# A two-layer encoder trunk on one core: the chunk loop pinned to a written order, with PSUM banks of their own for masked scores and copied keys

## The chip, the cores and the metric

The kernel runs on one core of a Trainium2 chip. The core has a matrix engine (TensorE, PE in the profile, its weight loads PEld), a vector engine (VectorE, DVE), a scalar engine (ScalarE, ACT), GpSimd (POOL) and SyncE (SP), which issues the DMAs. Each engine takes its instructions from a queue of its own, in order, and an instruction at the head of a queue that waits for another engine holds up everything behind it. The metric is the time of one execution on the device in microseconds (us). Three runs of the kernel before took 1314.47 to 1317.25 us, with a median of 1316.5.

## The reference

The input x has 1024 tokens of 1024 numbers. Layer 0 projects it once and feeds two branches. Branch A is a Conformer convolution (gate, depthwise convolution over 31 tokens, LayerNorm, swish). Branch B is RWKV-7 time mixing: 8 heads of 64, in both directions, with a state of 64 x 64 per head:

```python
def step(S, inp):
    r_t, w_t, k_t, v_t, kk_t, a_t = inp
    sa = jnp.einsum('dbhvk,dbhk->dbhv', S, -kk_t)
    S = (S * w_t[..., None, :] + sa[..., :, None] * (kk_t * a_t)[..., None, :]
         + v_t[..., :, None] * k_t[..., None, :])
    return S, jnp.einsum('dbhvk,dbhk->dbhv', S, r_t)
```

The results of the two directions are added, normalised per head (group norm), scaled, a bonus term is added, and each branch is multiplied with a gate. The two branches side by side go through one output projection, `l0_w_out`, of 1024 x 1024; its first 512 rows belong to the convolution branch and its last 512 rows to branch B. Then x becomes LayerNorm(alpha x + mixer(x)). Layer 1 is a bidirectional chunked gated linear attention with 4 heads, again with an output projection and a LayerNorm. Everything is in 32-bit floating point.

## The kernel before

**Stages.** `phase_a` projects x, does the convolution taps and prepares the operands of the recurrence, which it writes to DRAM (tensors `ak`, `br`, `vt`, that is `akd`, `brd` and `vtd` in the profile). `conv_norm` finishes branch A. The class `Delta` computes the recurrence in 16 chunks of 64 tokens. `mix0` normalises the result per head, projects it and finishes layer 0. `layer1` is the second layer.

**The recurrence in chunks.** For each chunk, direction d and pair of heads t (two heads e lie on the two halves of the partitions) a triangular system of 64 x 64 has to be inverted. `solve` and `system` build the systems in four batches of four chunks, `invert` inverts their 32 x 32 diagonal blocks by elimination (batch 2 on DVE, batch 3 on POOL, with transposes on DVE at L510, L530 and L531 and two copies on ACT at L535), and `join` combines the blocks of one chunk (L551, L556). Batches 2 and 3 are inverted within the chunk loop (`INVERT`).

`Delta.run` is the chunk loop. For chunk s it issues the loads of chunk s + 2 (`load`), the `chain` of chunk s, one or two joins, the `operands` of chunk s + 1, and `between(s)`. `operands` multiplies the chunk's keys with its queries: the tile `pk` (64 x 192 for each head: 64 columns that are the keys themselves, since q holds a unit matrix there, and 128 columns of scores) and the tile `pa`. DVE masks the scores of `pk` into `q` (L599), ACT copies the keys from the same tile (L600); of `pa`, DVE masks one half into `ga` (L602) and ACT copies the other into `at` (L603). `chain` then is a sequence of small matmuls: `pw` (L624), copied to `w` by ACT; `pu` (L630), copied to `u`; `pf`, the next state, which DVE multiplies with the decay into the top half of `rs` of the next chunk (L641); and `py`, the output, copied to `yst` and stored.

**Fill.** The output projection of the convolution branch is cut into 16 tiles (`ConvHalf`: 8 row tiles for each half of 512 columns; 12 matmuls `po` each, after a split of the input into a high and a low part, on ACT and POOL). Five (`EAGER`) run ahead of the loop, the others are put behind the chunks by `FILL`, two per chunk. The weights of a half (`owah`, `owal`) are staged in pieces of 256 KB through two buffers `ws` and split into a high part by ACT (L755) and a low part by DVE (L756) when the first tile of the half is written.

**After the loop.** `mix0` stages the other half of the output weights (`owbh`, `owbl`, eight pieces `ws`) and the first value block of layer 1 (`blk`, four pieces) through two buffers with the tag `owbs`. The function `by_head` in it takes its `hi` and `lo` tiles from the same two buffers. `rwkv` normalises one row tile: `yf + yb` on DVE (L898), two passes of `by_head` on PE, several steps on ACT and DVE, a product on POOL, and a split into `lh` and `ll`. The tiles are taken in the order 3, 4, 2, 5, 1, 6, 0, 7, since the middle ones need only the middle chunks of both directions. The SBUF pool of `mix0`'s weights (`m0w`) is allocated after the pools of the inversion (`bz`), of the convolution weights (`m0a`) and of the convolution tiles (`m0b`) have been released.

**What sets the order.** A scheduler orders the instructions of each engine from the order in which they are written, the dependencies and its own estimate of times; an instruction that it takes to be ready may be placed ahead of earlier written ones. `tc.keep_in_program_order(ins)` pins an instruction behind the instruction written before it on the same engine. In the kernel before this is used for the accumulating matmuls of `pf` and `py` and a few loads.

**PSUM.** Eight banks of 2 KB per partition: two for `pk`, systems and the first joins (`bmm`), one for `pa` (`bpa`), three for the chain (`bpc`), two for projection tiles and the later joins (`fps`).

Of the kernel before, what the change touches and what calls it, by code (L numbers as in the profile page):

```python
# [8 lines left out]
F32 = mybir.dt.float32  # L9
# [49 lines left out]
C_N = 928  # L59
# [13 lines left out]
def prog(tc, I, out, dbg=None):  # L73
# [42 lines left out]
    half = lambda h: Out(tc, E, I["wo0"][:, 0:NT, h * 512:h * 512 + 512], pw, "owa", 2)  # L116
# [4 lines left out]
    for s in range(4):  # L121
        delta.join(s)
# [7 lines left out]
    with tc.high_priority():  # L130
        for n in range(EAGER):
            conv.tile(0, n, nc.vector)
    rest = list(range(EAGER, 2 * KT))

    def fill(m):
        for n in rest[:m]:
            conv.tile(n // KT, n % KT)
        del rest[:m]

    def between(s):  # L140
        if s in INVERT:
            delta.invert(INVERT[s], bz)
        fill(FILL[s] if s < len(FILL) else 0)

    delta.run(between)
    fill(len(rest))
# [35 lines left out]
FILL = (0, 2, 2, 2, 2, 2, 2, 1)  # L182
# [269 lines left out]
class Delta:  # L452
# [8 lines left out]
    def __init__(self, tc, E):  # L461
# [3 lines left out]
        self.pm = pool(name="bmm", bufs=2, space=PSUM)  # L465
# [73 lines left out]
    def join(self, s):  # L539

        nc, pm = self.tc.nc, self.pm
# [4 lines left out]
        pool, tag = (pm, "mm") if s < 8 else (self.fp, "ps")  # L546
# [5 lines left out]
        for r0, r1 in rows:  # L552
            A.copy(xn[r1], ps[r1, 0])
        for u in range(U):
            for r0, r1 in rows:
                PE.matmul(ps[r0, 1, u], lhsT=xn[r1, u], rhs=xu[r1, u, 32:64], start=True, stop=True)  # L556
        for r0, r1 in rows:
            A.copy(xu[r0, :, 32:64], ps[r0, 1])

    def load(self, s):  # L560
# [7 lines left out]
        self.ops[s] = (ak, q)  # L568
# [8 lines left out]
    def operands(self, s):  # L577

        nc, cst = self.tc.nc, self.E["cst"]
        PE, V, A = nc.tensor, nc.vector, nc.scalar  # L580
        ak, q = self.ops[s]
        at = self.p2.tile([P, 2, NT, L], F32, name="at", tag="at")
        ga = self.p2.tile([P, 2, NT, L], F32, name="ga", tag="ga")
        self.ops[s] = (q, at, ga)
        for d in range(2):
            pa = self.pa.tile([P, NT, P], F32, name="pa", tag="pa")
            for h in range(2):
                pk = self.pm.tile([P, 2, 3 * L], F32, name="pk", tag="mm")
                ts = slice(2 * h, 2 * h + 2)
                for t in range(2):  # L590
                    for e, rw in enumerate(ROWS):
                        PE.matmul(pk[ROWS[1 - e], t], lhsT=ak[rw, d, 2 * h + t, 1], rhs=q[rw, d, 2 * h + t, e], start=True, stop=True)  # L592
                    for e, rw in enumerate(ROWS):
# [749 lines left out]
```

## Time and profile before

| what | value |
|---|---|
| median of three runs | 1316.5 us |
| the profiled execution | 1315.19 us |
| its span in the profile | 1313.3 us |
| granted clock of TensorE, mean | 0.955 |
| chunk loop | about 502 to 773 us |
| `mix0` after the loop | about 773 to 877 us |

A line of the profile names the line of the kernel, the engine, the operation, what is written and read (`out<-in`) with shapes, and how often. In a timeline the first two numbers are the start and the length in us; idle time of the engine ahead of an instruction, with what ended it, stands in brackets. In a list of waits the numbers are the total in us, the count and the longest. In a grouped line the numbers after the bar are the busy time in us, the mean of one in ns, and the idle time ahead with what ended it. A 32-bit matmul shows as two instructions.

### The profile page before, as it was taken

To read this page: it belongs to the slowest core of one execution; us is meant where nothing else is said; L and a number is where in the kernel's file an instruction comes from. 1 tells how busy PE (TensorE), PEld (TensorE's weight loads), DVE (VectorE), ACT (ScalarE), POOL (GpSimd) and SP (SyncE) were. 2 spreads that over 40 slices of the span, in tenths; PEclk is the share of its full clock that TensorE was granted. 3 is DMA by queue.
4 is the path that set the end of the run, shared out by engine and by line. 5 is a ranking of instruction groups with operands and counts; after the bars stand their busy time and mean duration, and the time that the engine had idled before them with its cause. 6 is when DMAs were issued, how large, how long until landed. Compare 5 with 4: busy or idle time off the path is not lost.

```text
span 1313.3 us, 26499 instructions
## 1 busy us (share of the span) xinstructions
PE 1200.0 (91%) x10824; PEld 986.1 (75%) x10824; DVE 861.1 (66%) x1435; ACT 583.2 (44%) x1165; POOL 431.5 (33%) x405
## 2 busy tenths in 40 slices
PE   7999998989998488599978998899999999999997
PEld 5887776767777357478857787777989999887785
DVE  5698999899835993252455779747685666442443
ACT  5545564645643424344345545346353524242221
POOL 1237857493826768201000013401020202010243
PEclk9999998989999688799989999899999999999999
DMA  6215343443798944247487656212111110131222
GB/s 222 65 49 142 123 135 114 121 135 114 216 265 225 228 134 130 57 116 194 127 240 176 171 149 198 95 61 81 33 33 33 41 41 16 33 97 49 112 97 80
DMA packets 203753, 155.92 MB, mean 119 GB/s; under 512 B 93132, under 2 KB 168268, under 8 KB 203376
## 3 DMA queue, kind: packets, MB, share of 16 engines
q1 hardware_dynamic: 203632, 154.24, 40.9%
q8 instruction: 85, 1.39, 0.5%
q14 instruction: 36, 0.29, 0.1%
HBM read 104.92 MB, written 49.28 MB: 117 GB/s over the span
## 4 chain that ended last, share of the span: by engine, by line
PE 52%; DVE 20%; DMA 10%; ACT 6%; issue 6%; POOL 4%; SPq 1%; POOLq 0%; DVEq 0%; ACTq 0%
PE ps L170 6%; PE ps L168 6%; PE ps L169 6%; PE po L168 4%; DVE acc L250 4%; PE po L169 4%; PE po L170 3%; DMA w<-w 2%; DMA ws<-wo 2%; PE psv L168 2%; PE psv L170 2%; PE psv L169 2%; PE po L1200 2%; PE pk L592 2%; PE pf L617 2%
## 5 line engine op out<-in xcount | busy, mean ns | idle before, releaser
L168 PE MATMUL ps<-xh,wh 128*128 128x512 f32 (+1 forms) x480 | 193.2, 405 | 10.4 <-ACT xh L755 6.3
L169 PE MATMUL ps<-xl,wh 128*128 128x512 f32 (+1 forms) x480 | 192.7, 402 | 0.4 <-DVE xl L756 0.4
L170 PE MATMUL ps<-xh,wl 128*128 128x512 f32 (+1 forms) x480 | 192.5, 402 | 0.1
L250 DVE SCALAR_TENSOR_TENSOR acc<-up,vec,acc 128x1024 f32<-128x1024 f32 x116 | 149.0, 1285 | 2.3
L168 PEld LDWEIGHTS ps<-xh,wh 128*128 128x128 f32 (+1 forms) x480 | 92.3, 192 | 33.8 <-ACT xh L755 6.8
L169 PEld LDWEIGHTS ps<-xl,wh 128*128 128x128 f32 (+1 forms) x480 | 92.7, 193 | 22.0 <-DVE xl L756 1.3
L170 PEld LDWEIGHTS ps<-xh,wl 128*128 128x128 f32 (+1 forms) x480 | 92.4, 192 | 21.6 <-DVE wl L756 0.6
L599 DVE TENSOR_TENSOR q<-pk,cst 64x256 f32<-64x256 f32 x128 | 53.5, 420 | 55.5 <-PE pk L592 37.6
L168 PE MATMUL ps<-x1h,w1h 128*128 128x512 f32 x224 | 88.9, 397 | 0.0
L170 PE MATMUL ps<-x1h,w1l 128*128 128x512 f32 x224 | 88.3, 394 | 0.0
L169 PE MATMUL ps<-x1l,w1h 128*128 128x512 f32 x224 | 88.3, 394 | 0.0
L793 DVE SCALAR_TENSOR_TENSOR xr<-xr,po 128x512 f32<-128x512 f32 x48 | 32.7, 682 | 71.6 <-PE po L170 70.7
L813 POOL TENSOR_TENSOR xr<-xr,lnr 128x1024 f32<-128x1024 f32 (+2 forms) x16 | 29.1, 1817 | 151.3 <-ACT xr L809 151.3
L1147 POOL TENSOR_TENSOR e<-zq,e 128x1024 f32<-128x1024 f32 x4 | 9.6, 2408 | 203.2 <-ACT e L1144 203.2
L756 POOL TENSOR_TENSOR wl<-w,wh 128x512 fp32r<-128x512 f32 (+1 forms) x30 | 44.3, 1475 | 90.4 <-ACT wh L755 81.6
L595 PE MATMUL pa<-q,ak 64*64 64x128 f32 x512 | 43.5, 294 | 25.4 <-ACT at L603 25.4
L592 PE MATMUL pk<-q,ak 64*64 64x192 f32 x512 | 58.3, 350 | 5.8 <-ACT q L600 5.8
L908 POOL TENSOR_TENSOR yf<-yf,gb 128x512 f32<-128x512 f32 x8 | 10.5, 1315 | 146.6 <-DMA ak<-akd 95.2
L168 PE MATMUL psv<-w1h,x1h 128*128 128x256 f32 x192 | 55.0, 286 | 1.1 <-DVE v1l L756 1.1
L170 PE MATMUL psv<-w1h,x1l 128*128 128x256 f32 x192 | 54.9, 286 | 0.0
L169 PE MATMUL psv<-w1l,x1h 128*128 128x256 f32 x192 | 54.8, 286 | 0.0
L755 ACT CAST wh<-w 128x512 fp32r<-128x512 f32 (+1 forms) x60 | 36.2, 605 | 37.7 <-PE ps L169 26.7
(350 smaller groups left out, 3254.3 us busy)
## 6 DMA issues: line engine op xcount, KB each, us to landing
w<-w SPq DMA_DIRECT2D x100, 256.0 KB, 3.1
brd<-br SPq DMA_DIRECT2D x16, 512.0 KB, 3.6
akd<-ak SPq DMA_DIRECT2D x16, 512.0 KB, 3.5
ak<-akd SPq DMA_DIRECT2D x16, 512.0 KB, 4.5
q<-brd SPq DMA_DIRECT2D x32, 256.0 KB, 4.9
vtd<-vt SPq DMA_DIRECT2D x32, 128.0 KB, 2.6
ws<-wo SPq DMA_DIRECT2D x16, 256.0 KB, 4.4
ab<-akd SPq DMA_DIRECT2D x16, 256.0 KB, 5.0
```

The costliest lines, as they stand in the source:

```text
L168: nc.tensor.matmul(ps, lhsT=lh, rhs=rh, start=first, stop=False)
L169: nc.tensor.matmul(ps, lhsT=lh, rhs=rl, start=False, stop=False)
L170: nc.tensor.matmul(ps, lhsT=ll, rhs=rh, start=False, stop=last)
L250: V.scalar_tensor_tensor(acc if i < KS - 1 else cv, up[:, i:i + T], w(i), acc, ALU.mult, ALU.add)
L592: PE.matmul(pk[ROWS[1 - e], t], lhsT=ak[rw, d, 2 * h + t, 1], rhs=q[rw, d, 2 * h + t, e], start=True, stop=True)
L595: PE.matmul(pa[rw, 2 * h + t], lhsT=ak[rw, d, 2 * h + t, 0], rhs=ur, start=True, stop=True)
L599: V.tensor_tensor(q[ro, d, ts, e, 64:], pk[ro, :, 64:], mask, ALU.mult)
L617: ins = PE.matmul(*args, **kw)
L755: nc.scalar.copy(hi, src)
L756: (eng or nc.vector).tensor_tensor(lo, src, hi.bitcast(F32), ALU.subtract)
L793: nc.vector.scalar_tensor_tensor(x[:, hs], x[:, hs], alpha, ps, ALU.mult, ALU.add)
L813: G.tensor_tensor(x[:, lo], x[:, lo], g[:, lo], ALU.mult)
```

## The change

**The written order.** Two small classes, `Pinned` and `Ordered`, wrap the matrix, vector and scalar engines so that each instruction issued through them is pinned. All of the chunk loop on these three engines goes through such wrappers: chain, scores, keys, joins, the projection tiles of the fill. SP and POOL instructions are not pinned, nor are those of `invert`. `chain`, `join` and `between` become generators, and `run` writes their parts interleaved.

**PSUM.** `operands` is replaced by `scores` (the 128 score columns `pk` and the tile `pa`, whose masks are now both on DVE, with a table that has ones in its first half, into one tile `ag`) and `keys` (the 64 key columns in a tile `pt`, copied by ACT). `pk`, `pa` and `pt` each take one of three banks of the pool `bmm`; the pool `bpa` goes. `pw` and `pu` become one tile for both directions, with one copy of 512 columns instead of two of 256.

**The fill.** `FILL` now has at most one tile per chunk, nine in all; two tiles are written after the loop, pinned, with the low part on DVE. A tile is begun in one chunk (loads, split), multiplied later in that chunk, and its sum is written in the next. The second half of the weights is staged two pieces at a time from chunk 3 to chunk 5 (`HALF`). The joins of chunks 4 to 7 take their bank from `fps` instead of `bmm`.

**After the loop.** The splits of the output weights and of the first value block in `mix0` are pinned too, behind what is written before them.

```diff
-        self.pm = pool(name="bmm", bufs=2, space=PSUM)
+        self.pm = pool(name="bmm", bufs=3, space=PSUM)
...
+    def scores(self, s, d):
+        cst, (PE, V, _) = self.E["cst"], self.engines
+        ak, q, ag = self.ops[s]
+        pk = self.pm.tile([P, NT, P], F32, name="pk", tag="mm")
+        pa = self.pm.tile([P, NT, P], F32, name="pa", tag="mm")
+        for t in range(NT):
+            for e, rw in enumerate(ROWS):
+                PE.matmul(pk[ROWS[1 - e], t], lhsT=ak[rw, d, t, 1], rhs=q[rw, d, t, e, 64:], start=True, stop=True)
+            for e, rw in enumerate(ROWS):
+                ur = q[rw, d, t, e].rearrange("p (w i) -> p w i", w=3)[:, 0::2]
+                PE.matmul(pa[rw, t], lhsT=ak[rw, d, t, 0], rhs=ur, start=True, stop=True)
+        for e in range(2):
+            ro = ROWS[1 - e]
+            V.tensor_tensor(q[ro, d, :, e, 64:], pk[ro], cst[ro, C_MS:C_MS + P].unsqueeze(1).broadcast_to([64, NT, P]), ALU.mult)
+        V.tensor_tensor(ag[:, d], pa, cst[:, C_AC:C_AC + P].unsqueeze(1).broadcast_to([P, NT, P]), ALU.mult)
+
+    def keys(self, s, d):
+        PE, _, A = self.engines
+        ak, q, _ = self.ops[s]
+        ps = self.pm.tile([P, NT, L], F32, name="pt", tag="mm")
+        for t in range(NT):
+            for e, rw in enumerate(ROWS):
+                PE.matmul(ps[ROWS[1 - e], t], lhsT=ak[rw, d, t, 1], rhs=q[rw, d, t, e, 0:64], start=True, stop=True)
+        for e in range(2):
+            A.copy(q[ROWS[1 - e], d, :, e, 0:64], ps[ROWS[1 - e]])
...
         for s in range(NCH):
+            more, nxt = s + 2 < NCH, s + 1 < NCH
+            other = between(s, fixed)
+            joins = [self.join(j, fixed) for j in (2 * s + 4, 2 * s + 5) if j < NCH]
+            go = lambda g: next(g, None)
+            chain = self.chain(s)
+            if more:
+                self.load(s + 2)
+            go(chain)                 # pw, copy to w
+            go(other)                 # inversion, sum of the last tile, split of the next
+            go(chain)                 # pf, first half
+            if nxt:
+                self.scores(s + 1, 0)
+            go(chain)                 # pu, copy to u
+            if nxt:
+                self.keys(s + 1, 0)
+            for j in joins[:1]:
+                go(j)
+            go(chain)                 # py, first half
+            go(chain)                 # pf, second half, decay
+            if nxt:
+                self.scores(s + 1, 1)
+            for j in joins[:1]:
+                go(j)
+            go(chain)                 # py, second half, copy to yst
+            if nxt:
+                self.keys(s + 1, 1)
+            for j in joins[1:]:
+                go(j)
+            go(other)                 # projection tile
+            for j in joins[1:]:
+                go(j)
+            for _ in other:
+                pass
...
+class Pinned:
+    def __init__(self, tc, engine):
+        self.tc, self.engine = tc, engine
+    def __getattr__(self, name):
+        return lambda *args, **kw: self.tc.keep_in_program_order(getattr(self.engine, name)(*args, **kw))
+
+class Ordered:
+    def __init__(self, tc):
+        self.tensor, self.vector, self.scalar = (Pinned(tc, e) for e in (tc.nc.tensor, tc.nc.vector, tc.nc.scalar))
+        self.gpsimd, self.sync = tc.nc.gpsimd, tc.nc.sync
...
-FILL = (0, 2, 2, 2, 2, 2, 2, 1)
+FILL = (1, 1, 1, 0, 0, 0, 1, 1, 1, 1, 1, 1, 0, 0, 0, 0)
+HALF = 3
...
     delta.run(between)
-    fill(len(rest))
+    fixed = Ordered(tc)
+    for n in rest:
+        conv.tile(n // KT, n % KT, fixed, fixed.vector)
...
-    proj = Out(tc, E, I["wo0"][:, NT:], wbp, "owb", 2)
+    fixed = Ordered(tc)
+    proj = Out(tc, E, I["wo0"][:, NT:], wbp, "owb", 2, nc=fixed)
...
-            split(nc, res[0][:, k:k + 2], res[1][:, k:k + 2], w)
+            split(nc if i else fixed, res[0][:, k:k + 2], res[1][:, k:k + 2], w)
```

(The words after `#` in the loop are added here.)

More of the change, by code (lines that the diff above doesn't have):

```diff
@@ L121, in prog @@
     for s in range(4):
-        delta.join(s)
+        for _ in delta.join(s):
+            pass
     for j in range(FIRST + 1, 2 * NT):
@@ new lines, in chain @@
+        for d, t, e in units:
+            PE.matmul(ps[ROWS[1 - e], d, t], lhsT=q[:, d, t, e, 64:128], rhs=rs[:, d, t, e], start=True, stop=True)
+        A.copy(f(w), f(ps))
+        yield
+        pf = s + 1 < NCH and tile("pf")
+        if pf:
+            for d, t, e in units:
+                PE.matmul(pf[ROWS[e], d, t], lhsT=q[:, d, t, e, 0:64], rhs=rs[:, d, t, e], start=d + t == 0, stop=False)
+        yield
+        ps = tile("pu")
+        for d, t, e in units:
+            ro = ROWS[1 - e]
+            PE.matmul(ps[ROWS[e], d, t], lhsT=xa[ro, d, t], rhs=w[ro, d, t], start=True, stop=True)
@@ L649, in chain @@
-        A.copy(yst.rearrange("p d t i -> p (d t) i"), ps)
-        nc.sync.dma_start(self.E["y"][s], yst)
+            PE.matmul(py[ROWS[e], d, t], lhsT=u[ROWS[e], d, t], rhs=ag[ROWS[e], d, t, 64:], start=False, stop=d + t == NT)
+        A.copy(f(yst), f(py))
+        self.tc.nc.sync.dma_start(self.E["y"][s], yst)
+        yield
     def run(self, between):
         tc, nc = self.tc, self.tc.nc
+        fixed = Ordered(tc)
+        self.engines = fixed.tensor, fixed.vector, fixed.scalar
         self.p2 = tc.alloc_tile_pool(name="b2", bufs=2, reuse_waits="tile", side="right")
-        self.pa = tc.alloc_tile_pool(name="bpa", bufs=1, space=PSUM, reuse_waits="tile")
@@ L759, with __init__ @@
 class Out:
-    def __init__(self, tc, E, w, pw, tag, stages=2, room=None):
-        nc = tc.nc
+    def __init__(self, tc, E, w, pw, tag, stages=2, room=None, later=None, nc=None):
+        nc = nc or tc.nc
         _, self.n, self.cols = w.shape
@@ L774, in __init__, with stage, fetch, cut @@
             for i, h in enumerate(hs):
-                ws = room.tile([P, 512], F32, name="gup") if room else pw.tile([P, 512], F32, name="ws", tag=tag + "s", bufs=stages)
-                nc.sync.dma_start(ws, w[:, k, h])
-                split(nc, *self.w[k][i], ws)
+                steps = self.stage(nc, w[:, k, h], self.w[k][i], pw, tag + "s", stages, room)
+                if later is None:
+                    steps[0]()
+                    steps[1](nc)
+                else:
+                    later.append(steps)
+    def stage(self, nc, src, dst, pw, tag, stages, room):
+        tile = []
+        def fetch():
+            if not tile:
+                tile.append(room.tile([P, 512], F32, name="gup") if room else pw.tile([P, 512], F32, name="ws", tag=tag, bufs=stages))
+                nc.sync.dma_start(tile[0], src)
+        def cut(nc):
+            fetch()
+            split(nc, *dst, tile[0])
+        return fetch, cut
     def norm(self, rows, pw):
@@ L1300, in layout @@
     cst[:, C_DM:C_DM + 32] = p % 32 < i[:, 0:32]
+    cst[:, C_AC:C_AC + P] = np.where(i < 64, 1, p % 64 <= i % 64)
     r["cst"] = cst
```

174 lines of the change are left out of this document (79 added, 95 removed).

## The prediction

> **What bounds the kernel now.** I read the page first, then the stages, then the waits inside the chunk loop. The page says that TensorE is busy nearly everywhere:
>
> ```profile
> span 1313.3 us, 26499 instructions
> PE 1200.0 (91%) x10824; PEld 986.1 (75%) x10824; DVE 861.1 (66%) x1435; ACT 583.2 (44%) x1165; POOL 431.5 (33%) x405
> ```
>
> That average covers stages with different limits, so here is the table by stage (the columns after the stretch are its length, then busy time and instructions of PE, weight load, DVE, ACT and POOL, then granted clock, DMA share and GB/s). The loop's first scores start at 502 and its last instructions end at 773; the second half of layer 0 runs from there to 877.
>
> ```profile
> 502.00:538.60 36.60, 21.28 (x469) 16.93 (x463) 10.76 (x19) 10.38 (x29) 29.26 (x56) 0.73 0.25 71
> 538.60:648.30 109.70, 108.83 (x2224) 87.31 (x2226) 44.46 (x95) 48.82 (x144) 9.47 (x8) 0.98 0.47 130
> 648.30:714.50 66.20, 51.49 (x1072) 43.28 (x1064) 35.35 (x78) 28.57 (x78) 0.00 (x0) 0.95 0.79 209
> 714.50:773.00 58.50, 56.79 (x1173) 44.86 (x1171) 40.52 (x94) 35.87 (x98) 4.18 (x4) 0.97 0.61 154
> 773.00:843.00 70.00, 60.87 (x320) 50.84 (x319) 61.92 (x123) 32.18 (x65) 27.72 (x17) 0.98 0.53 169
> 843.00:877.00 34.00, 30.96 (x193) 27.37 (x194) 16.09 (x36) 11.45 (x28) 3.52 (x4) 0.90 0.14 52
> ```
>
> The loop is bound by PE except in two places: the first row (15.3 us idle) and the third (14.7 us idle). DVE has more than half of its time free in the loop; from 773 to 843 it is the fullest engine, 61.9 of 70. The waits of the loop name the two holes:
>
> ```profile
> ACT q L600 <- DVE q L599: 39.8, 73, 2.3
> ...
> PE pa L595 <- ACT at L603: 16.4, 2, 15.3
> ...
> ACT owbh L755 <- DMA ws<-wo: 15.3, 6, 6.0
> ...
> PE pw L624 <- DVE q L599: 5.6, 6, 1.8
> ```
>
> The first hole is one wait: two copies of the last inversion stand in ACT's queue ahead of the copy that PE needs, and wait for POOL's elimination to end.
>
> ```profile
> 536.04 2.11 ACT L535 COPY xa<-xa 32x1024 f32<-32x1024 f32 x2 [14.37 <-DVE xa L531]
> ```
>
> The second is the staging of the output weights (casts to owbh) that hold ACT up for a DMA in the middle of the loop. The 39.8 us in which ACT waits for DVE on one score tile, because both read the same bank, cost PE little: it waited for those masks 5.6 us in all.
>
> **The change, part by part.** *The matmuls of a chunk.* The row below is a chunk late in the loop: it starts at 726.50 and the next at 738.45, 11.95 us, of which three matmuls of the next stage (the two of L891 and L890 in this fence and one more) take near 0.36 each, 1.1, so 10.85.
>
> ```profile
> 726.50 0.80 PE L624 MATMUL pw<-rs,q 128*64 128x64 f32 x18
> 727.23 0.50 PE L891 MATMUL pv<-lo,one 128*128 128x512 f32 x1
> 727.56 0.40 PE L890 MATMUL pc<-hi,cen 128*128 128x512 f32 x1
> ...
> 728.26 0.87 PE L592 MATMUL pk<-q,ak 64*64 64x192 f32 x8
> 729.06 0.33 PE L624 MATMUL pw<-rs,q 128*64 128x64 f32 x2
> ...
> 732.80 0.69 PE L617 MATMUL pf<-rs,q 128*64 128x64 f32 x16
> 733.41 0.68 PE L617 MATMUL pf<-u,at 64*64 64x64 f32 x16
> ...
> 735.48 1.15 PE L617 MATMUL py<-q,rs 128*64 128x64 f32 x32
> 736.56 0.97 PE L617 MATMUL py<-ga,u 64*64 64x64 f32 x26
> ...
> 738.45 0.80 PE L624 MATMUL pw<-rs,q 128*64 128x64 f32 x18
> ```
>
> Starts give the rates: 32 matmuls of 64 columns in 736.56 - 735.48 = 1.08 us, 34 ns each; eight of 192 columns alone in 0.80, 100 ns each. After the change a chunk has 224 matmul instructions of 64 columns (pw, pu, pf, py, and 32 for the keys, which leave the wide pk): 7.6 us. The 64 of 128 columns (scores) lie between 34 ns (2.2 us) and two thirds of the 100 ns (4.3 us); written in one order, four quadrants in turn, I take 40 ns, 2.5 us, near the low end because the rate of the narrow ones is mostly issue. Sixteen pf matmuls between two changes of tile shape take 0.61 us where 16 at 34 ns would take 0.54: a change costs 0.07 us. The old order has some 20 changes a chunk, the written one four to eight: 0.4 us. Together 10.5 us, 0.35 less than that chunk; the keys' own matmuls take back most of what fewer changes give. The Trainium skill, TensorEngine Tiling (Array Packing), Key Properties, says that switching the tiling mode drains TensorE; the trace agrees, with those 0.07 us. By that rule the sum stands as it is; if the 0.07 us were no drain and stayed with the matmuls, a chunk would be about 1 us longer and the sum 15 us later.
>
> *Joins and convolution tiles.* A half join and a projection tile, by the starts of what follows:
>
> ```profile
> 564.60 0.69 PE L556 MATMUL pj<-xa,xn 32*32 32x32 f32 x32
> 565.23 0.68 PE L630 MATMUL pu<-w,xa 64*64 64x64 f32 x16
> ...
> 571.88 0.50 PE L168 MATMUL po<-owah,lh 128*128 128x512 f32 x1
> ...
> 574.84 0.45 PE L624 MATMUL pw<-rs,q 128*64 128x64 f32 x8
> ```
>
> 0.63 us a half, 1.26 a join; 2.96 us a tile. The new loop holds 12 joins (15 us), 9 tiles (26.6), 15 full chunks (157.5), a last one without scores and state (5.5) and the first scores (3.5): 208 us. To this I add idle time: 10 of the 15.3 us at the inversion (ACT's pinned work after step 2 is placed behind the inversion's copies, and those are themselves free to be placed early, as before; behind them in ACT's queue stand the copies of w, u and the keys, and PE waits for those; ends 0 and 15), and 6 us of short waits, the 1.7 in 58.5 us of the fourth row scaled up. So 224 us where 271 were: **the loop ends 47 us earlier, near 726** (ends 37 and 62).
>
> *DVE and ACT in a chunk.*
>
> ```profile
> L599 DVE TENSOR_TENSOR q<-pk,cst 64x256 f32<-64x256 f32 x128 | 53.5, 420 | 55.5 <-PE pk L592 37.6 <-ACT q L600 16.3
> L793 DVE SCALAR_TENSOR_TENSOR xr<-xr,po 128x512 f32<-128x512 f32 x9 | 6.2, 685 | 17.9 <-PE po L170 17.9
> ```
>
> Six masks of 512 elements at 0.69 replace eight q masks and two ga masks at 0.42: 4.1 us for 4.2. With four decays (1.7) DVE needs 5.8 us in 10.5 and stays hidden; the copies of w and u, merged to 512 elements, take some 0.6 us and lie under pf's first half and the scores (over 3 us of PE). Their banks no longer change hands between DVE and ACT; what this frees is in the short waits. Three banks instead of two for the early systems, the larger table and the earlier residual load I cost at nothing: DVE's eliminations set the pace there. If that cover is gone it is a microsecond or two, either way.
>
> *What leaves the loop.* This part decides. The splits of the output weights (8) and of the first value block (4) are now pinned on ACT and DVE behind the last two projection tiles, and those behind the last chunk. In the old run the first weight load went out as soon as the last projection tile had read its weights, which lie in the same memory:
>
> ```profile
> 652.03 0.39 PE L170 MATMUL po<-owah,ll 128*128 128x512 f32 x1
> ...
> 653.09 1.02 SPq L776 DMA_DIRECT2D ws<-wo  x2
> ```
>
> No load had started earlier though SP had room, so I take it that loads must wait for that tile again, now the last thing after the loop. First the tail: ACT split, DVE split, 2.96 of PE, sum, the second split pinned behind that sum, 2.96 of PE: 10 us. That is an estimate from 2 x 2.96 and five short ACT and DVE steps. Then 12 staged pieces of 256 KB through two buffers. The nearest row is the same pattern on a quiet machine, eight pieces for layer 1:
>
> ```profile
> 877.13 15.92 SPq L1036 DMA_DIRECT2D w<-w  x8
> ...
> 896.58 0.69 DVE L756 TENSOR_TENSOR w1l<-w,w1h 128x512 fp32r<-128x512 f32 x1 [1.22 <-ACT w1h L755]
> ```
>
> 877.13 to 897.27 is 20 us, 2.5 a piece: 30 us. The head normalisation (rwkv in the second half) uses the same two buffers for its hi and lo parts, so it starts only then; its six loads a tile go with it, but land while the weights are staged. One tile's chain, two by-head passes through ACT, DVE and PE, took 17 us in the busy loop (734.52 to 751.5); with the engines to itself I take three quarters of that, 13 us.
>
> ```profile
> 731.09 1.12 DVE L907 SCALAR_TENSOR_TENSOR yf<-yf,vec,bv 128x128 f32<-128x128 f32 x4
> ...
> 734.52 0.69 DVE L898 TENSOR_TENSOR yf<-yf,yb 128x512 f32<-128x512 f32 x1 [1.08 <-DMA yb<-yd]
> ...
> 750.85 0.68 DVE L756 TENSOR_TENSOR ll<-yf,lh 128x512 fp32r<-128x512 f32 x1
> ...
> 773.42 0.40 PE L168 MATMUL po<-owbh,lh 128*128 128x512 f32 x1
> ```
>
> Before, the output projection began at 773.42, directly at the loop's end, with four tiles normalised. Now it begins 10 + 30 + 13 = **53 us after the loop** (ends 32, if the hi and lo parts get their buffers first, and 62). After that DVE has 3.4 more tiles to normalise than before, at 4.5 us (five instructions near 0.69 and the four of 1.12 together): 15 us on the engine that filled 61.9 of 70 us there; with 8 us free, **12 us** later (7 to 15).
>
> The long idle stretch has a price of its own: after the old 4.90 us wait the first eight pk matmuls took 1.54 us where 0.87 is usual.
>
> ```profile
> 675.58 1.54 PE L592 MATMUL pk<-q,ak 64*64 64x192 f32 x8 [4.90 <-ACT q L600]
> ```
>
> The Trainium skill, TensorE: Matmul & The Clock Gate, Part 1, has the array at half its clock after some 3.4 us idle until it has been busy as long; the trace agrees (0.73 granted in the first row of the loop). By that rule the sum would be 2 us higher; I leave it inside the range.
>
> **The sum.** -47 + 53 + 12 = +18 us on the profiled execution's 1315.2 (span 1313.3 and 1.9 around it; the median of the runs is 1.3 higher): 1333.
>
> **The rivals.** *Handover overlapped, faster.* If the hi and lo parts take buffers as they come free and only the eight output weights are needed, projection starts 32 us after the loop and DVE adds 7: -8, 1307; without the inversion's stall -18, 1297. For it: DVE and ACT are half empty while pieces land. Against: the loads are older in the program and fill both buffers at once. It decides from a handover below about 40 us with the loop as forecast. *No stall at the inversion.* Chunks 0 and 1 with joins and tiles are 33 us of PE, just the time that POOL needs up to 536; ordered well they cover it: 8 to 10 us less, 1324. *The written order itself waits.* From the end of pf to pw's second half PE has 3.4 us of work (scores 1.25, py's second half 1.08, keys 0.54, pw's first half 0.54); DVE needs four decays and two masks in that time, 3.06 us and the hand-offs. It just fits, and PE may no longer take other work meanwhile: 1 us a chunk is 15 us, 1348. That the order gains nothing on PE (10.85 a chunk, not 10.5) belongs here, +5 us.
>
> **How the numbers follow.** Forecast 0.42 (1333, its own range 1325 to 1342), overlapped handover 0.27, no stall 0.18, waiting order 0.13. Within 0.2% (2.6 us, about what a measurement of this kernel can tell from no change) lies a little of the second and third, 0.08; faster 0.30; slower 0.62. Leaving out a tenth at each end: 1296 to 1352.
>
> **What would show it.** Right: chunk starts (pw) 10 to 11 us apart without tiles and joins; no owbh casts between chunks; the last yst copy near 726; then PE nearly empty for some 45 us while ws lands, with the first po on owbh near 779; layer 1's start 15 to 20 us later than 877. Wrong: owbh casts or yf adds ahead of the last chunk, the loop ending before 705, or a gap behind it under 40 us.

## The result, and the profile after

The changed kernel takes 1331.5 us (median of four runs, 1326.4 to 1333.5) against 1315.5 beside it (1312.4 to 1317.3): 1.0119 times as long, 95% interval 1.0083 to 1.0154. The profiled execution took 1331.9, 16.7 more than the one before, where 18 were forecast. Its page:

```profile
span 1330.1 us, 27402 instructions
PE 1166.5 (88%) x11336; PEld 974.5 (73%) x11336; DVE 860.7 (65%) x1373; ACT 563.2 (42%) x1037; POOL 431.9 (32%) x403
PE   7999998889989575799997068799999999999997
```

TensorE works 33.5 us less than before and the run is longer: the "06" in the 40 slices is a stretch from 732 us on in which it stands still (slices of 33.3 us). The stages (columns as in the prediction): the rest of the loop from its second half chunk of scores, the handover, and the output projection of the second half; the last row is the projection stage of the kernel before, between the same two projection matmuls.

```profile
495.10:718.60 223.50, 190.90 (x5372) 174.23 (x5372) 102.34 (x172) 78.07 (x176) 43.64 (x72) 0.92 0.51 131
718.60:774.70 56.10, 12.53 (x32) 6.57 (x32) 18.67 (x32) 16.07 (x27) 1.62 (x1) 0.61 0.57 175
774.70:873.20 98.50, 82.31 (x384) 67.86 (x385) 81.09 (x160) 45.42 (x90) 34.01 (x21) 0.86 0.47 143
```

```profile
773.40:853.40 80.00, 70.77 (x372) 59.75 (x371) 67.61 (x134) 33.83 (x70) 29.08 (x19) 0.96 0.49 158
```

So the 16.7 us are: loop ended 54.8 earlier (773.4 to 718.6), a handover of 56.1 where there was none, 18.5 more in the projection stage, and 3 won back behind it. The waits of the changed kernel, from the loop to the first projection, show the two places where TensorE stands, and the loads behind the second:

```profile
PE pu L738 <- ACT w L738: 21.0, 2, 20.3
...
PE pc L993 <- ACT hi L818: 34.7, 1, 34.7
ACT owbh L738 <- DMA ws<-wo: 30.1, 7, 10.1
```

*The loop's hole* is the old one, and longer. ScalarE's queue, then what TensorE waited for:

```profile
536.20 2.11 ACT L552 COPY xa<-xa 32x1024 f32<-32x1024 f32 x2 [22.13 <-DVE xa L548]
538.34 0.74 ACT L738 COPY xa<-pj 32x256 f32<-32x256 f32 x2
539.10 0.58 ACT L738 COPY w<-pw 128x512 f32<-128x512 f32 x1
```

```profile
539.73 1.97 PE L738 MATMUL pu<-w,xa 64*64 64x64 f32 x32 [20.25 <-ACT w L738]
```

The copies of the last inversion stand ahead of the second chunk's copy of w. They end at 538.3; before the change they ended at 538.15. GpSimd sets that time (VectorE, whose transposes the copies read, waits 19.9 us for its elimination), so whatever TensorE saves ahead of it only lengthens the hole.

*A chunk* late in the loop, without tiles or joins, now takes 702.84 - 693.29 = 9.55 us, of which TensorE is busy 9.14:

```profile
693.29 0.80 PE L738 MATMUL pw<-rs,q 128*64 128x64 f32 x18
...
695.99 0.33 PE L738 MATMUL pk<-q,ak 64*64 64x128 f32 x2
...
696.91 1.10 PE L738 MATMUL pu<-w,xa 64*64 64x64 f32 x32
697.84 0.63 PE L738 MATMUL pt<-q,ak 64*64 64x64 f32 x16
...
702.84 0.80 PE L738 MATMUL pw<-rs,q 128*64 128x64 f32 x18
```

```profile
693.30:702.80 9.50, 9.14 (x291) 8.72 (x288) 5.67 (x11) 3.18 (x8) 0.00 (x0) 1.00 0.51 136
```

*The handover*, in order of time: last output of the loop, first load of a weight, its cast, then SyncE's queue ahead of the seventh load, that load's cast, the first head normalisation, and the first projection:

```profile
718.01 0.58 ACT L738 COPY yst<-py 128x512 f32<-128x512 f32 x1 [1.56 <-PE py L738]
...
726.47 0.81 SPq L852 DMA_DIRECT2D ws<-wo  x2
...
729.76 1.22 ACT L738 CAST owbh<-ws 128x512 fp32r<-128x512 f32 x2 [10.13 <-DMA ws<-wo]
...
739.47 1.64 SPq L985 DMA_DIRECT2D gb<-gbd  x1
...
743.39 0.45 SPq L852 DMA_DIRECT2D ws<-wo  x1
...
747.90 0.62 ACT L738 CAST owbh<-ws 128x512 fp32r<-128x512 f32 x1 [5.24 <-DMA ws<-wo]
...
760.49 0.62 ACT L818 CAST hi<-yf 128x512 fp32r<-128x512 f32 x1 [0.81 <-DVE blk L738]
761.16 0.79 PE L993 MATMUL pc<-hi,cen 128*128 128x512 f32 x1 [34.72 <-ACT hi L818]
...
774.72 0.80 PE L184 MATMUL po<-owbh,lh 128*128 128x512 f32 x1 [0.98 <-ACT lh L818]
```

Three parts one after the other: two convolution tiles to 726.5, staging to 760.5, one normalisation to 774.7. The wait of 34.7 us ends when a buffer of the staged weights comes free for hi.

### The profile page after: what moved, and what is told of

Read it like the earlier page. It is cut to its first block, busy times and chain, and to the rows that moved or that the text cites. A ratio compares the mean times of both kernels' runs of the same rounds, so it can differ in the third digit from the quotient of the medians.

```text
span 1330.1 us, 27402 instructions
## 1 busy us (share of the span) xinstructions
PE 1166.5 (88%) x11336; PEld 974.5 (73%) x11336; DVE 860.7 (65%) x1373; ACT 563.2 (42%) x1037; POOL 431.9 (32%) x403
## 5 line engine op out<-in xcount | busy, mean ns | idle before, releaser
L738 DVE TENSOR_TENSOR q<-pk,cst 64x512 f32<-64x512 f32 x64 | 44.0, 687 | 33.3 <-PE pa L738 26.6
L884 DVE SCALAR_TENSOR_TENSOR xr<-xr,po 128x512 f32<-128x512 f32 x37 | 25.3, 684 | 54.2 <-PE po L186 54.2
L185 PE MATMUL psv<-w1l,x1h 128*128 128x256 f32 x192 | 54.8, 286 | 0.0
L818 ACT CAST wh<-w 128x512 fp32r<-128x512 f32 (+1 forms) x60 | 36.2, 606 | 42.0 <-PE ps L185 25.3
L1011 POOL TENSOR_TENSOR yf<-yf,gb 128x512 f32<-128x512 f32 x8 | 12.3, 1536 | 124.7 <-DVE yf L1010 102.8
L819 POOL TENSOR_TENSOR ll<-ya,lh 128x512 fp32r<-128x512 f32 x9 | 11.4, 1270 | 125.8 <-ACT lh L738 125.8
L186 PE MATMUL po<-owch,ll 128*128 128x512 f32 x128 | 50.8, 398 | 0.0
```

What stands on the lines that cost most here:

```text
L185: nc.tensor.matmul(ps, lhsT=lh, rhs=rl, start=False, stop=False)
L186: nc.tensor.matmul(ps, lhsT=ll, rhs=rh, start=False, stop=last)
L738: return lambda *args, **kw: self.tc.keep_in_program_order(getattr(self.engine, name)(*args, **kw))
L818: nc.scalar.copy(hi, src)
L819: (eng or nc.vector).tensor_tensor(lo, src, hi.bitcast(F32), ALU.subtract)
L884: (nc or self.tc.nc).vector.scalar_tensor_tensor(x[:, hs], x[:, hs], alpha, ps, ALU.mult, ALU.add)
```

## The experiments

Twelve kernels, each timed against the kernel before on its own chip (its medians there: 1314.2 to 1316.3). Marks of the profiled execution, in us: start of the first pw, end of the loop's last copy (yst), start of the first and of the last projection matmul on owbh; then span, median, and the ratio to the kernel before with its interval.

| run | pw | yst | first po | last po | span | median | ratio |
|---|---|---|---|---|---|---|---|
| before | 505.2 | 773.4 | 773.4 | 853.4 | 1313.3 | 1315.5 | 1 |
| after | 498.1 | 718.6 | 774.7 | 873.2 | 1330.1 | 1331.5 | 1.0119 [1.0083, 1.0154] |
| e1 late copies | 494.8 | 708.1 | 763.8 | 859.9 | 1318.2 | 1321.3 | 1.0058 [1.0031, 1.0086] |
| e2 tiles early | 499.9 | 735.3 | 771.5 | 864.2 | 1321.2 | 1324.9 | 1.0068 [1.0045, 1.0092] |
| e3 written staging | 499.4 | 737.4 | 751.8 | 849.7 | 1306.3 | 1309.2 | 0.9946 [0.9922, 0.9970] |
| e4 no pins | 492.1 | 711.2 | 761.0 | 858.4 | 1315.2 | 1317.2 | 1.0009 [0.9986, 1.0031] |
| e5 own buffers | 496.7 | 719.0 | 751.0 | 847.5 | 1303.7 | 1310.4 | 0.9964 [0.9934, 0.9995] |
| e6 grouped | 500.4 | 745.8 | 800.9 | 897.7 | 1354.3 | 1354.9 | 1.0302 [1.0263, 1.0342] |
| e7 two early banks | 495.6 | 712.8 | 767.8 | 865.5 | 1322.9 | 1329.7 | 1.0115 [1.0066, 1.0164] |
| e8 combined | 495.7 | 715.5 | 723.4 | 815.2 | 1273.0 | 1274.7 | 0.9680 [0.9643, 0.9718] |
| e9 shared banks | 504.5 | 736.8 | 792.5 | 888.8 | 1344.5 | 1344.7 | 1.0211 [1.0172, 1.0250] |
| e10 shared, no pins | 494.5 | 732.0 | 778.3 | 876.9 | 1331.1 | 1329.5 | 1.0105 [1.0067, 1.0143] |
| e11 inversion alone | 498.9 | 699.4 | 754.3 | 851.9 | 1309.7 | 1311.6 | 0.9961 [0.9935, 0.9988] |
| e12 no pins, tiles early | 490.1 | 732.1 | 738.8 | 838.0 | 1294.8 | 1297.5 | 0.9869 [0.9831, 0.9907] |

**The hole at the inversion.** e1 pins the end of the inversion one step later:

```diff
+        if s == 2:
+            late.append(delta.invert(3, bz, fixed))
+            next(late[0])
+        if s == 3:
+            next(late[0])
...
+        yield
+        if fixed:
+            nc, V = fixed, fixed.vector
         V.memset(z.rearrange("p i j -> p (i j)")[:, ::33], 1.0)
```

> The end of the last inversion (one memset, two transposes, two copies on ScalarE) is pinned one step later, in step 3, where its result is still early; the elimination itself stays where it is. Theory: in the changed kernel these copies stand in ScalarE's queue ahead of the copy of w in the second chunk, and TensorE waits 20.25 us for that copy. The wait goes. What is late next: the low halves of the next two convolution tiles, which GpSimd computes behind the elimination (to 534), so the first tile's third matmul waits about 6 us instead. Net 14 us: loop 210 us instead of 223.5, 1318 us in all, with the handover after the loop unchanged at 56 us. Rival A, nothing is late next: 20 us, 1312. Rival B, TensorE waits for GpSimd's elimination by another way (the joins need it at once): no change, 1331.

The loop ended 10.5 us earlier, 10 us in the median. TensorE's wait for w is gone, and the next thing is late, as expected, by 8.3 us where 6 were expected:

```profile
532.41 0.80 PE L749 MATMUL po<-owah,ll 128*128 128x512 f32 x1 [8.28 <-POOL ll L830]
```

e11 makes the edit of e1 and takes that away too:

```diff
-        ahead = [conv.begin(n // KT, n % KT, fixed) for n in rest[:FILL[s]]]
+        ahead = [conv.begin(n // KT, n % KT, fixed, fixed.vector if s < 3 else None) for n in rest[:FILL[s]]]
```

> The changed kernel with the late copies of the last inversion, and with the low halves of the tiles of steps 0 to 2 on VectorE instead of GpSimd, so that nothing TensorE needs stands behind the elimination. Theory (the 8.3 us left in the run with late copies alone is GpSimd's queue): the second chunk takes 14 to 15 us instead of 36, the loop is 20 us shorter, handover as before: 1311. Rival (VectorE is held by something else of the inversion): second chunk over 18 us, 1317 or more.

1311.6: the second chunk takes 15.4 us instead of 36.1, and the loop from the first pw 200.5 instead of 220.5. So 10 us of the median were ScalarE's copies ahead of `w` (e1), and 10 more the low halves behind the elimination in GpSimd's queue (e11). With this alone the change is 0.4% faster than the kernel before instead of 1.2% slower.

**The handover.** e2 moves the tiles:

```diff
-FILL = (1, 1, 1, 0, 0, 0, 1, 1, 1, 1, 1, 1, 0, 0, 0, 0)
+FILL = (1, 1, 1, 0, 0, 0, 2, 2, 2, 2, 0, 0, 0, 0, 0, 0)
```

> All eight convolution tiles of the second half are done two a step in steps 6 to 9, so none is left behind the loop and the memory of their weights is free from step 10 on; the splits of the output weights stay pinned behind the loop. Theory (memory and the last tiles hold the first loads, the pins hold the rest): the loop gets two tiles longer (5.9 us, to 229), the 8.6 us tail behind it goes, the first two pieces have landed by then (3 to 6 us less), the other ten are still staged one after the other. First output projection about 44 us behind the loop instead of 56, in all 5 to 9 us faster, 1324. Rival A, the memory alone was the hold: the pieces are staged inside the loop, the projection starts within 15 us of the loop, 1296 or less. Rival B, the convolution's tail was hidden anyway: within 3 us of 1331.

6.6 us faster, within the expected 5 to 9 (the interval just touches that of the changed kernel), but by other sums. The handover is 36.2 us, not 44: the tail of 8 is gone and staging takes 25 us instead of 34. The loop from the first pw takes 235.4 us, 14.9 more, not 6. TensorE's work in it grew by 8; the rest is waiting, 2.9 us of it in one chunk, where the loads of the head normalisation, let go by the freed memory, meet the operands of a chunk:

```profile
695.00:708.80 13.80, 10.92 (x292) 10.32 (x290) 5.91 (x12) 3.29 (x8) 0.00 (x0) 0.88 1.11 287
```

13.8 us for a chunk without tiles, with all DMA engines busy at 287 GB/s. The longest wait of TensorE there, 2.0 us, has no releaser in the profile, so that the loads cause it is likely and not shown. The memory alone was not the hold of the staging, since ten pieces still waited for the pins. e12 makes this edit and that of e4 below, no pins:

> The run without pins, and the eight convolution tiles of the second half two a step in steps 6 to 9 as in the run with early tiles, so that neither the memory nor a pin holds the staging back. Theory (the handover is made by the late tiles and kept by the pins: with both gone the casts move into the loop, as in the kernel before): all twelve casts stand in ScalarE's queue between the copies of w of three chunks about step 10; TensorE waits there for the loads 10 to 15 us, as it did 14.7 us before the change; the projection starts 15 to 18 us behind the loop instead of 50: 1317 - 33 + 12 = 1296. Rival (a load in the loop costs as much as one behind it): the stall is 25 us or more, 1310 to 1320.

1297.5 for 1296. All twelve casts stand in the loop again, and ScalarE waits 24 us there for the pieces. The two chunks concerned take 15.6 and 25.6 us instead of about 10, and TensorE stands 17 us in them, more than the 10 to 15 expected; the handover is 6.7 us, less than the 15 to 18.

```profile
ACT owbh L818 <- DMA ws<-wo: 15.0, 8, 5.1
...
ACT blk L818 <- DMA ws<-w: 9.0, 4, 5.3
```

```profile
669.60:695.20 25.60, 15.17 (x288) 13.98 (x288) 12.49 (x22) 8.64 (x16) 0.00 (x0) 0.64 0.91 242
```

So the late tiles made the handover and the pins kept it; neither alone explains it. e3 keeps the pins, has the tiles early as e2 has, and writes the staging into the order:

```diff
+        if s == 10:
+            conv.pk.release()
+            pw.release()
+            bz.release()
+            pre.append(weights0(tc, I, E, delta, pieces))
+        else:
+            for fetch, cut in pieces[:2]:
+                cut(fixed)
+                pieces.pop(0)
+        for fetch, cut in pieces[:2]:
+            fetch()
...
```

(`weights0` takes the memory of the weights and lists the twelve pieces.)

> As the kernel with the tiles done early, and the twelve pieces (eight of output weights, four of the first value block) are put into the written order: from step 10 on two are fetched in a step and split in the next, the last two behind the loop; the hi and lo parts of the head normalisation still use the same two buffers. Theory (the handover is staging plus the first normalisation, one after the other): the loop is 6 us longer for two tiles and stays bound by TensorE; behind it remain about 3 us of staging and 14 us of normalisation, so the projection starts 17 to 20 us behind the loop instead of 56: 1331 + 6 - 38 = 1299. Rival A, loads in the loop are late as they were in the kernel before (14.7 us of TensorE idle for six casts): the loop grows by 10 to 20 us and the sum is 1310 to 1320. Rival B, the projection is bound by VectorE whatever its start: less than half of the 38 us is kept, 1315.

1309.2, between theory (1299) and the rivals. The handover fell to 14.4 us, better than the 17 to 20. The loop's end came 18.8 us later instead of 6. Part of that is the chunk from 693.2 to 711.1, 17.9 us, where the normalisation's loads again take the DMA engines and a weight was late in spite of its chunk of lead:

```profile
703.47 0.62 ACT L747 CAST owbh<-ws 128x512 fp32r<-128x512 f32 x1 [6.93 <-DMA ws<-wo]
```

e5 leaves tiles and staging as the change has them and takes away the shared buffers:

```diff
+    tc.keep_in_program_order(A.preload_act_table_set(LNEXP))
...
-        hi, lo = (wbp.tile([P, NT * P], F32R, name=nm, tag="owbs", bufs=2) for nm in ("hi", "lo"))
+        hi, lo = (wbp.tile([P, NT * P], F32R, name=nm, tag="hl", bufs=2) for nm in ("hi", "lo"))
...
```

> In the changed kernel the hi and lo parts of the head normalisation get two buffers of their own instead of those of the staged weights (the low part of the normalised tile has two buffers instead of three to make room), and the table of logarithm and exponential is loaded ahead of the staging. Theory (of the 56 us behind the loop the last 14 are the first normalisation, which waits for the last staged piece only for its buffer): two tiles are normalised while the pieces land, the projection starts with the last output weight, at 756 instead of 774.7, 18 us earlier, and two tiles of VectorE work (9 us) leave the stage that VectorE fills: 1305 in all. Rival A, only the start moves: 1313. Rival B, what is normalised early holds up the splits behind it in ScalarE's queue: the start moves by less than 8 us, 1324 or more.

1310.4: 21 us faster for two buffers and a table loaded earlier. The start moved by 23.7 us (751.0; it did not even wait for the last weight, cast at 753.66), the stage shrank by 2 us, not 9: nearer to rival A. This is the prediction's "handover overlapped", which it priced at 1307.

**What makes the chunk short.** e4 takes every pin away:

```diff
-        self.tensor, self.vector, self.scalar = (Pinned(tc, e) for e in (tc.nc.tensor, tc.nc.vector, tc.nc.scalar))
+        self.tensor, self.vector, self.scalar = tc.nc.tensor, tc.nc.vector, tc.nc.scalar
```

> Nothing is pinned in the loop, the convolution tail or the staging; the banks and the sequence in which the program states the work stay as changed. Theory (the chunk is short because tile shapes change less often, and that comes from the way the work is stated with banks of its own, not from the pins): a chunk without tiles and joins stays at 9.5 us against 10.85 to 12 before; the copies of the last inversion fall one chunk further back in ScalarE's queue, so the wait of 20 us shrinks to about 7; the handover stays at 56 because the last tiles are still last: 1318 to 1322. Rival, the pins make the chunk short: chunks of 10.5 to 12 us, the loop 15 to 35 us longer, 1340 or more.

1317.2 and chunks as short as with pins:

```profile
680.80:690.50 9.70, 9.36 (x292) 8.82 (x290) 5.87 (x11) 3.25 (x8) 0.00 (x0) 1.00 0.48 123
690.50:699.50 9.00, 8.95 (x290) 8.58 (x288) 5.17 (x11) 3.15 (x8) 0.00 (x0) 1.00 0.10 35
```

```profile
542.42 1.98 PE L651 MATMUL pu<-w,xa 64*64 64x64 f32 x32 [10.00 <-ACT w L640]
```

The hole is 10.0 us instead of 20.25 (7 expected), and the last tiles slid into the loop, so the handover lost 6 us. The pins themselves cost 14 us here (the intervals 0.9986 to 1.0031 and 1.0083 to 1.0154 do not meet) and gave the chunk nothing. e9 keeps the pins and undoes the banks; e10 makes this edit and that of e4:

```diff
-        pk = self.pm.tile([P, NT, P], F32, name="pk", tag="mm")
+        A = self.engines[2]
+        pks = [self.pm.tile([P, 2, 3 * L], F32, name="pk", tag="mm") for h in range(2)]
...
+                V.tensor_tensor(q[ro, d, ts, e, 64:], pks[h][ro, :, 64:], cst[ro, C_MS:C_MS + P].unsqueeze(1).broadcast_to([64, 2, P]), ALU.mult)
+                A.copy(q[ro, d, ts, e, 0:64], pks[h][ro, :, 0:64])
...
```

> The written order is kept and the banks are undone: in the changed kernel the scores and the copied keys come again from one matmul of 192 columns into a shared bank, two tiles a bank, with four masks on VectorE and four copies on ScalarE for each half chunk; the 32 key matmuls of a chunk are gone. Theory (the banks are what lets the written order run): TensorE saves 32 x 29 ns = 0.9 us a chunk, but masks and copies of one bank follow each other (0.42 and 0.37 us, four pairs and one mask of 0.69, 3.9 us), and only 0.9 us of TensorE work lies between the second half's scores and the next chunk's w: TensorE waits some 2 to 3 us a chunk. Chunks of 11 to 12 us instead of 9.5, 20 to 35 us in all, 1350 to 1365. Rival (the order alone makes the chunk short, the banks only cost the 32 matmuls): chunks of 8.6 to 9.5 us, 1317 to 1331.

> As the kernel with shared banks, and nothing is pinned: both halves of the change are undone but the sequence in which the program states the work. Theory (banks matter, pins don't): chunks of 10.5 to 12 us as in the kernel before, 15 to 25 us more than the run without pins with banks of its own: 1332 to 1345. Rival (without pins other work fills the waits of the shared bank): chunks within 0.5 us of 9.5, 1310 to 1320.

With pins the banks are worth 13.2 us (1344.7 against 1331.5). Without pins the difference is 12.3 (1329.5 against 1317.2), but there the hole at the inversion is another too: in e10 the second chunk takes 36.9 us, with two waits of TensorE of 13.3 and 5.8, against the one wait of 10.0 in e4. So not all of the 12.3 is the shared bank. Both runs lie below their theories: late chunks take 9.1 to 10.7 us, not 11 to 12, and in e9 TensorE waits 3.6 us in three of them together, not 2 to 3 in each. Masks and copies of one bank follow each other, as thought, but work on TensorE covers most of it (e9, 560 to 720 us):

```profile
ACT q L735 <- DVE q L735: 82.1, 94, 3.4
```

The price is paid earlier, from the third to the seventh chunk, four of which hold joins (the changed kernel, then e9): TensorE stands 11.2 us there instead of 5.1, and the granted clock is lower.

```profile
552.50:621.40 68.90, 63.85 (x1979) 58.90 (x1976) 33.30 (x57) 31.03 (x74) 1.28 (x1) 0.95 0.55 137
```

```profile
558.40:638.60 80.20, 69.00 (x1822) 62.54 (x1816) 36.43 (x77) 32.83 (x94) 1.27 (x1) 0.85 0.47 115
```

The Trainium skill, PSUM — Partial Sum Buffer, PSUM bank collisions raise a hardware error, says that VectorE and ScalarE reading one bank and quadrant at once collide and must be kept apart by a semaphore; the trace shows the keeping apart (94 such waits with shared banks, none in the loop with banks of their own), and no collision.

And e10, with neither pins nor banks of their own, has late chunks of 9.1 to 9.9 us where the kernel before took 10.85, with the same number of matmul instructions (10824). Much of the difference stands in the rows of the scores. In the kernel before, the `pa` of one direction ran by themselves (16 in 1.02 us), and the `pk` too (8 in 0.80, in the prediction's fence): 2.6 us for the 32 of a direction. In e10 the two tiles run through each other, 32 in 1.35 us:

```profile
717.06 1.09 PE L595 MATMUL pa<-q,ak 64*64 64x128 f32 x16
718.08 0.45 PE L624 MATMUL pw<-rs,q 128*64 128x64 f32 x6
```

```profile
692.75 0.38 PE L607 MATMUL pk<-q,ak 64*64 64x192 f32 x2
692.77 0.43 PE L610 MATMUL pa<-q,ak 64*64 64x128 f32 x4
...
694.10 1.10 PE L648 MATMUL pu<-w,xa 64*64 64x64 f32 x32
```

What is left of the change in e10 is the restated chain: both directions in one tile and one copy, and the sequence of the statements. It shortens a late chunk by taking matmuls together; which of its parts makes the scheduler do so no run separates, and in the kernel before head normalisation also ran in these chunks.

**The width of a score.** A matmul on 64 rows into 64 partitions uses one quadrant (64x64) of the array. The changed kernel's scores go to the four quadrants in turn: `pk` to two of them, `pa` to the other two. e6 writes the 64 score instructions of a chunk quadrant by quadrant:

```diff
-        for t in range(NT):
-            for e, rw in enumerate(ROWS):
+        for e, rw in enumerate(ROWS):
+            for t in range(NT):
                 PE.matmul(pk[ROWS[1 - e], t], lhsT=ak[rw, d, t, 1], rhs=q[rw, d, t, e, 64:], start=True, stop=True)
...
```

> In the changed kernel the 64 score matmuls of a chunk (128 columns each) are written quadrant by quadrant, four in a row into the same quarter of the array, instead of the four quarters in turn; the same matmuls, banks and masks. In the changed kernel one takes 29 ns, as much as one of 64 columns, where the prediction took 40. Theory A (the width is hidden because the other three quarters take the next matmuls meanwhile): a quarter needs up to 116 ns for its own, so 64 of them up to 5.6 us longer a chunk; with some of that overlapped between groups 30 to 80 us in all, 1360 to 1410. Theory B (29 ns is the rate of issue and the width costs nothing at all): 1331, within 4 us.

23 us longer, below theory A's lower end and far from B. The chunk takes 11.1 us instead of 9.55; the scores are 2.1 us longer, and the short wait of before is covered:

```profile
719.72 1.25 PE L739 MATMUL pk<-q,ak 64*64 64x128 f32 x13
...
721.69 0.27 PE L739 MATMUL pu<-w,xa 64*64 64x64 f32 x2
```

32 scores from 719.72 to 721.69 are 62 ns each, where the changed kernel's 32 from 695.99 to 696.91 are 29 ns. The rows between show why: the changed kernel first, where four instructions start within some 0.02 us, one in each quadrant, and the next four 0.11 us later; then e6, where each of two quadrants starts one every 0.11 us:

```profile
696.15 0.28 PE L738 MATMUL pk<-q,ak 64*64 64x128 f32 x2
696.16 0.28 PE L738 MATMUL pa<-q,ak 64*64 64x128 f32 x2
696.26 0.28 PE L738 MATMUL pk<-q,ak 64*64 64x128 f32 x2
```

```profile
720.81 0.27 PE L739 MATMUL pk<-q,ak 64*64 64x128 f32 x1
720.86 0.27 PE L739 MATMUL pa<-q,ak 64*64 64x128 f32 x1
720.92 0.27 PE L739 MATMUL pk<-q,ak 64*64 64x128 f32 x1
```

So the width is not free: a quadrant takes 0.11 us for 128 columns, and four at work hide it. The narrow `pu` comes to 29 ns as well (32 in 0.93 us, 696.91 to 697.84), but it uses only two quadrants, so one takes 0.06 us for 64 columns. Whether narrow matmuls in all four would be faster no run tests. The Trainium skill, TensorE: Matmul & The Clock Gate, Back-to-back issue gap, gives an issue floor of about 25 ns up to 64 columns and some 56 ns for 128; the trace does not agree with it for these 32-bit instructions within one quadrant, with 58 ns for 64 columns and 110 for 128.

**The early start.** e7 gives the early systems two banks again:

```diff
-        self.pm = pool(name="bmm", bufs=3, space=PSUM)
+        self.pm = pool(name="bmm", bufs=2, space=PSUM)
...
+        self.pt = tc.alloc_tile_pool(name="bpt", bufs=1, space=PSUM, reuse_waits="tile")
...
```

> In the changed kernel the early systems and joins have two PSUM banks again; the third bank holds only the copied keys in the loop, so inside the loop every score and key sits in a bank as in the changed kernel. Theory (the loop starts 7 us earlier, second chunk's w at 498.1 against 505.2 for the first pw, because of the third bank): the first pw falls back to 503 to 506 and the run takes 1336 to 1339. Rival (the start comes from the way the loop's first work is stated): first pw within 2 us of 498, 1331.

(The two times in that text are those of the first pw after and before the change.) The first pw came at 495.6 and the time is that of the changed kernel. The third bank is not the cause of the earlier start; what is stays open, and it did not matter, since the hole behind it ends when GpSimd is done.

**Together.** e8 makes the edits of e3, e11 and e5 and loads the table at step 10:

```diff
+    tc.keep_in_program_order(tc.nc.scalar.preload_act_table_set(LNEXP))   # in weights0
```

> The written staging, the late copies of the last inversion with the low halves of the next two tiles moved to VectorE, the table loaded at step 10, and buffers of its own for the normalisation. Theory (the three losses are separate): the staging kernel's 1309 less 20 us for the inversion (no new wait now, since no low half stands behind the elimination on GpSimd) less 5 us for the buffers: 1284. Rival A, the earlier loop meets later loads and a part of the inversion's gain is lost: 1292 to 1300. Rival B, VectorE with two more halves becomes the bound in the first chunks: 1300 or more.

1274.7 us, 0.968 of the kernel before (0.9643 to 0.9718), 9 us better than expected. Alone the three parts gave 22, 20 and 21 us, 63 in all; together they give 57:

```profile
714.93 0.59 ACT L758 COPY yst<-py 128x512 f32<-128x512 f32 x1 [0.31 <-PE py L758]
...
723.35 0.80 PE L199 MATMUL po<-owbh,lh 128*128 128x512 f32 x1 [2.64 <-ACT lh L838]
```

```profile
723.40:815.20 91.80, 77.57 (x376) 63.57 (x377) 79.83 (x157) 43.16 (x86) 35.37 (x21) 0.90 0.50 149
```

The handover is 8 us, and the projection stage is still 92 us long, with VectorE at 79.8, where it was 80 before the change: what is left of the loss is there.

## Why the prediction was right, step by step

*The sum.* That 18 were forecast and 16.7 came is in part luck. The loop ended 54.8 us earlier for 47, the handover was 56.1 for 53, the stage behind it 18.5 longer for 12, and 3 were won back behind it where nothing was forecast: errors of -7.8, +3.1, +6.5 and -3. Some 7 us of the first are an earlier start of the loop (first pw at 498.1 for 505.2), for which the prediction has no term. The mechanism, a shorter loop and a handover that costs more than the loop gains, came as forecast.

*The loop, -47: right in its sum, by two errors that cancel.* It was put at 208 us of work and 16 of waiting; it took 190.9 and 32.6 (without the first half chunk of scores, which lies ahead of that stretch).

- The chunk was sized at 10.5 us and took 9.5; over 15.5 chunks that is 15.5 of the 17 us of work too many. The mis-sized terms are the scores, 40 ns where 29 was measured, and the narrow matmuls, 34 ns where 29 was. The 34 came from a run of 32 that begins with a change of tile shape: in the changed kernel `py` behind such a change takes 1.08 us (698.41 to 699.49) and `pu` without one 0.93. So a change costs some 0.15 us, not 0.07, and the prediction counted a part of it twice. Its reason for the scores, a rate that is mostly issue, is not what e6 shows: a quadrant needs time by the width, and four of them work at once. That the sequence in which the work is stated saves much of it (e10), and the pins nothing (e4), it did not see.
- The idle time at the inversion was taken at 10 us, between ends of 0 and 15; it was 20.25, outside them. The step that failed is the upper end: it took the old wait as the most, though GpSimd fixes the end of the hole and the loop's earlier and faster beginning only moves its start.
- The other waits were taken at 6 us and were 12.

That the copies of w and u and the hi lo casts would be the things held up, and by which copies, was right (e1, e11). "The written order itself waits" did not happen: between the chunks TensorE waits 0.36 us for a mask. The cost of nothing for three early banks held (e7).

*The handover, +53: 56.1.* Tail 8 (10 forecast), staging 34 (30), normalisation 14.2 (13). The staging ran over where SyncE's queue had loads of the head normalisation ahead of a weight: the seventh load was issued at 743.39, and its cast waited 5.24 us. The prediction had let those loads go along free of charge. First po on owbh at 774.7 for "near 779"; the gap, the empty stretch and the missing casts in the loop are as it said, and e2, e3, e5 and e12 each shorten the part they take away.

*VectorE afterwards, +12: 18.5.* VectorE's work grew by 13.5 us (67.6 to 81.1), near the 15 of the prediction. What failed is taking 8 us of free time off: the idle time of the stage did not shrink, it grew from 12.4 to 17.4 us. Why it grew is not settled; TensorE's by-head matmuls moved there too and its clock was lower.

*The clock.* The same by-head matmul took 0.40 us in the old loop and 0.79 in the empty stretch (761.16); the granted clock was 0.61 in the handover and 0.86 in the stage behind it, 0.96 before. It was half from 730.5 to 778.3, full again 3.6 us after the first projection, and half once more from 792.0, behind new waits of TensorE for the head normalisation:

```profile
730.50:778.30 47.80, 9.77 (x16) 5.11 (x17) 18.06 (x33) 15.89 (x26) 1.62 (x1) 0.50 0.57 168
...
792.00:802.20 10.20, 6.98 (x19) 5.09 (x20) 9.81 (x22) 5.76 (x12) 5.37 (x4) 0.50 0.63 169
```

By its mean, the stage had some 27 us at half clock (twice 0.14 of 98.5) where it had 6 before. The Trainium skill, TensorE: Matmul & The Clock Gate, Part 1, has half clock end once the array has been busy for a window of some 3.4 us; the trace agrees, with those 3.6 us. So the 2 us that the prediction drew from that rule fit the start of the stage; the later stretches of half clock, which come of waits inside the stage, it left out. They may be part of the 6.5 us by which the last term was short; no run separates them.

Layer 1's first loads go out at 893.62, 16.5 us later than 877.13, within the 15 to 20 that the prediction asked for:

```profile
893.62 10.79 SPq L1139 DMA_DIRECT2D w<-w  x6
```

## What to carry to other kernels

A written order fixes the good and the bad: here it pinned staging and last tiles behind the loop and copies ahead of work they were not due for, and cost 14 us, while the short chunk came from the sequence in which the work is stated, with matmuls for different quadrants side by side, and the banks paid off in the chunks with joins. Before pinning, list for each queue what stands at both ends of the pinned part and what it waits for; weights for the next stage want their memory free and their fetches one or more steps ahead inside the loop. And a wait whose end another engine sets grows by whatever is saved ahead of it.

## What the runs showed of the hardware

A 64x64 quadrant of the array takes a 32-bit matmul instruction of 64 columns in 0.06 us and one of 128 in 0.11 (two in turn for `pu`, 696.91 to 697.84; e6, 720.81 to 720.92), and the quadrants work beside each other: four in turn give 29 ns an instruction of 128 columns, grouped by quadrant it is 62 ns. A change between tile shapes costs some 0.15 us, an estimate from `py` (1.08 us) and `pu` (0.93). Behind a long half-empty stretch the clock was full again 3.6 us after the first projection; the mean of 0.86 in that stage comes of later stretches at half clock.
